# One-hots without factors, rows in two parts, and a router term that no longer crosses GpSimd

## The chip, the cores and the metric

One core of a Trainium2 chip runs the whole kernel; nothing is shared with another core. The metric is the device time of one execution in microseconds, and what is shown is the median of three runs. A profile belongs to one further execution of its own.

## The reference

A single layer of a diffusion backbone over 256 tokens of width 1024, all in float32. First an attention and a spatial-gating branch, joined by an output projection; then 32 experts, of which each token uses four.

```python
x_mid = x + gt1 * rms_norm(mix, g_post_mix[l])            # mix: attention | gating, @ w_out
h2 = modulate(rms_norm(x_mid, g_pre_ffn[l]), sh2, sc2)
logits = xt @ w_router + b_router                         # (256, 32)
top_logits, top_idx = lax.top_k(logits, 4)
gates = jax.nn.softmax(top_logits, axis=-1)
...
gu = xb @ w_gate_up[e] + b_gate_up[e]                     # xb: the rows of expert e
gate = jnp.minimum(gate, 7.0); up = jnp.clip(up, -7.0, 7.0)
act = (up + 1) * gate * jax.nn.sigmoid(1.702 * gate)
y_rows = (act @ w_down[e] + b_down[e]) * row_gate
y = jax.ops.segment_sum(y_rows, row_tok)                  # back to tokens
x_new = x_mid + gt2 * rms_norm(y, g_post_ffn[l])
```

All expert weights are read from HBM in every execution: 12.58 MB for each expert, about 403 MB in all.

## The kernel before, in words

**The part ahead of the experts** (0 to about 203 us) has its order written out by hand: `PLAN` is a list of words, each of which issues the next piece of a step (a generator). `broadcasts` (word `bcast`) spreads four rows of constants over the 128 partitions with GpSimd's partition broadcast. `router_terms` (word `rterms`) multiplies the shift `sh2` with the router's weights `wr` into one row (tile `brt` in PSUM), adds the router's bias into `brow`, and has GpSimd spread that row over the partitions (SBUF tile `brt`). `bparts` is a chain of small GpSimd steps that splits the experts' biases into parts (`braw`, `bgu`). `ra` is the inverse root of the attention rows' mean square: the matmul `oss` sums the squares, `rav` takes it over, and GpSimd works out the root. The output projection's results (`wo`) are scaled by `ra` on VectorE into `yacc`, which then frees `wo`'s PSUM bank.

**The experts** run in a loop `for e in range(NE)`. Their weights come through a ring of ten slots of SBUF (`slot`, `load_more`), six loads of 2 MB for each expert, issued on SyncE's queue (SP) as slots come free. One expert has 64 row slots. Two experts share a gather and a combine:

- `pair_one_hots` writes for 2 x 64 slots a one-hot matrix `oh` of tokens by slots, and `ohg`, the same with the gates in place of ones. In `oh` the ones are replaced by `zx`, the inverse root of the token's mean square.
- `gather_pair` (at the odd expert) multiplies the token rows `xs` by `oh` in float32, eight blocks of 128 columns, two token halves each, into `gx`, and `modulate` makes `xT` of it.
- `gu_chunk` (four for each expert) is the gate and up product, `swiglu` the activation (`g`, `sg`, `u`), `to_ff` the transposition `aT`, and `down` the product `py`, which is copied into `ye`, half by ScalarE and half by VectorE.
- `turn` (at the even expert) transposes `ohg` into `ohT` (`slots_to_partitions`, PSUM bank 2, the bank that `py` uses behind it) and combines the pair before: `combine` multiplies `ohT` with `ye` (`cb`, four float32 matmuls) and `add_y` adds into `yacc`.

TensorE runs its instructions in program order: at the even expert the pieces are `ohT`, `cb`, `aT`, the biases, `py`. An expert with more than 64 rows takes a branch (`rows_left`) through `more_start`, `more_chunk` and `more_down`; with these inputs that happens twice, at about 442 and 949 us. The last pair is handled apart (`project`, `add_up`), and the residual rows `xs` are added at the end.

Matmuls on float32 data leave two records each in the trace; those on data declared `FR` (float32r: the same 32 bits, one pass) leave one.

Of the kernel before, what the change touches and what calls it, by code (L numbers as in the profile page):

```python
# [20 lines left out]
P = 128  # L21
# [24 lines left out]
PLAN = """  # L46
first first bcast first@5 first first first split0 xin00@2 xin01@7 xin01 mod0@0 xin00 split0 xin10@3 first xin10
split0 mod0 mod0@7 split0 acc@6 bias mod0 bias bias bias bias bias split0 mod0 xin11@7 bias proj0 mod0 ada2 xin11
# [34 lines left out]
def kernel(  # L83
# [115 lines left out]
    load(vrow, vecs)  # L199
    xs = keep.tile([P, 2, D], F32, name="xs")  # L200
    for t in range(2):
# [662 lines left out]
    brt = pre.tile([P, NE], F32, name="brt")  # L864
    gt1 = keep.tile([P, D], F32, tag="ye", name="gt1")

# [295 lines left out]
    def modulate(xT, pb, k0, nk, w):  # L1162
# [3 lines left out]
        tt(xT[:, k0:k0 + nk, :], xT[:, k0:k0 + nk, :], bc(sh2[:, k0:k0 + nk].unsqueeze(2), shp), ADD, eng=G)  # L1166

    def one_hots(e, s0, oh, ohg):
        for t in range(2):
            if s0 == 0:  # L1170
                if oh(t) is not None:
                    ts(oh(t), iota[:, 0:oh(t).shape[-1]], pos1[:, t, e:e + 1], zx[:, t:t + 1], ALU.is_equal, MUL)
                ts(ohg(t), iota[:, 0:ohg(t).shape[-1]], pos1[:, t, e:e + 1], gate[:, t, e:e + 1], ALU.is_equal, MUL)
            else:
                w = ohg(t).shape[-1]
                ts(oh(t), iota[:, 0:w], float(s0), pos1[:, t, e:e + 1], ADD, ALU.is_equal)
                ts(ohg(t), oh(t), gate[:, t, e:e + 1])
                ts(oh(t), oh(t), zx[:, t:t + 1])

    def pair_one_hots(p):  # L1180
        oh = None if p == 0 else mt("oh", [P, 2, P])
        ohg = mt("ohg", [P, 2, P])
        for j in range(2):
            c = slice(SL * j, SL * j + SL)
            one_hots(2 * p + j, 0, lambda t: oh[:, t, c] if oh is not None else None, lambda t: ohg[:, t, c])
        return oh, ohg

    def gather_pair(oh):
        xT = mt("xT", [P, KD, P])
# [53 lines left out]

    def down(w, aT, ye):
# [26 lines left out]
    def more_start(e, s0, i, xT, pgu):  # L1271
        ohs = mt("oh", [P, 2, 2, SM])
        oh, ohg = ohs[:, 0], ohs[:, 1]
        one_hots(e, s0, lambda t: oh[:, t, :], lambda t: ohg[:, t, :])
        pb = bank(4, "gx")
        for k in range(KD):
            for t in range(2):
                PE.matmul(pb[:, SM * k:SM * k + SM], lhsT=xs[:, t, P * k:P * k + P], rhs=oh[:, t, :],
                          start=t == 0, stop=t == 1)
        modulate(xT, pb, 0, KD, SM)  # L1280
# [97 lines left out]

    def project(c0, n, j, w, aT, ye, b):

# [5 lines left out]
        yield  # L1386
        rows = ye[SL * j:SL * j + SL]
        S.copy(rows[:, c0:c0 + n], py[0][0:64, 0:n])
        V.tensor_copy(out=rows[:, c0 + n:c0 + 2 * n], in_=py[1][64:128, 0:n])
        yield  # L1390

    def add_up(c, i, ohT, ye, yg, b):
        for t in range(2):
            pb = bank(b + t, "cb")[:, 0:c.stop - c.start]
            PE.matmul(pb, lhsT=ohT[:, t, :], rhs=ye[:, c], start=True, stop=True)
            add_y(t, c, pb)
# [38 lines left out]
    ye = ohT = None  # L1435
    counts_of = {}
# [7 lines left out]
    def turn(p, banks):  # L1444
# [7 lines left out]
        return next(turned), keep.tile([P, D], F32, tag="ye", name=f"ye{p}")  # L1452

# [5 lines left out]
    for e in range(NE):  # L1459
# [14 lines left out]
        for c in range(4):  # L1474
# [4 lines left out]
            if c == 1 and last:  # L1479
                aT0 = to_ff(u0, scr[:, 0:512].rearrange("p (q s) -> p q s", q=4))  # L1480
                ohT, ye = turn(p, (6, 7, 0, 1))
            if c == 2 and not last:
                counts_of[e + 1] = count(e + 1, counted)
        if e == NE - 2:
            scr = slot(order[cursor[0] % NSLOT], "scr")
            cursor[0] += 1
            w0, more0, cv0 = w, more, cv
            continue
# [4 lines left out]
        if j == 0:  # L1493
            ohT, ye = turn(p, (4, 5, 6, 7))
        elif not last:
# [3 lines left out]
        if last:  # L1499

            first = project(0, 512, 0, w0, aT0, ye, 0)
            next(first)
# [8 lines left out]
        down_rest(e, w, more, cv)  # L1511
        down(w, aT, ye[SL * j:SL * j + SL])
        load_more(2)
# [83 lines left out]
```

## Time and profile before

| | |
|---|---|
| median of 3 runs | 1160.65 us (1160.21 to 1161.82) |
| profiled execution | 1159.75 us |
| its span, first to last instruction | 1157.9 us |
| mean granted TensorE clock | 0.966 of 2.4 GHz |
| PE busy | 1066.3 us (92%) |
| VectorE (DVE) / ScalarE (ACT) / GpSimd (POOL) busy | 343.6 / 150.1 / 110.4 us |
| DMA | 446.21 MB, 385 GB/s over the span, 425 to 428 GB/s in its flat stretches |

The span's ends, 1.85 us in all, belong to the execution but to no instruction. All engines' shares are averages over a part with little DMA, a long part in which both DMA and PE are nearly full, and a tail after the last weights. A record line gives the start, the busy time, engine, source line, operation, output <- inputs, shape and how many instructions it groups; what stands in brackets is the idle time ahead of it and what ended it. `L117` is the recording helper that issues nearly every instruction, so the tiles' names tell the places apart.

### The profile page before, as it was taken

To read this page: it belongs to the slowest core of one execution; us is meant where nothing else is said; L and a number is where in the kernel's file an instruction comes from. 1 tells how busy PE (TensorE), PEld (TensorE's weight loads), DVE (VectorE), ACT (ScalarE), POOL (GpSimd) and SP (SyncE) were. 2 spreads that over 40 slices of the span, in tenths; PEclk is the share of its full clock that TensorE was granted. 3 is DMA by queue.
4 is the path that set the end of the run, shared out by engine and by line. 5 is a ranking of instruction groups with operands and counts; after the bars stand their busy time and mean duration, and the time that the engine had idled before them with its cause. 6 is when DMAs were issued, how large, how long until landed. Compare 5 with 4: busy or idle time off the path is not lost. (4 is left out here: it accounts for less than half of the span.)

```text
span 1157.9 us, 14247 instructions
## 1 busy us (share of the span) xinstructions
PE 1066.3 (92%) x5653; PEld 526.6 (45%) x5653; DVE 343.6 (30%) x763; ACT 150.1 (13%) x308; POOL 110.4 (10%) x199
## 2 busy tenths in 40 slices
PE   6998979999999997999999999989998988999985
PEld 5865536343535443444453535343434352353534
DVE  4698534112121321322222121212121221312123
ACT  4654112111000000000000000000000000100011
POOL 2235252000000000000000000000000000000001
PEclk9998988999999998999999999999999998899998
DMA  9976866999999999989999999999999999899961
GB/s 375 369 282 247 352 218 234 408 428 424 425 426 427 425 426 428 424 354 426 428 424 428 421 428 423 426 426 425 426 426 426 426 426 428 359 430 423 423 256 38
DMA packets 36574, 446.21 MB, mean 385 GB/s; under 512 B 4081, under 2 KB 4321, under 8 KB 6657
## 3 DMA queue, kind: packets, MB, share of 16 engines
q1 hardware_dynamic: 36450, 444.47, 92.0%
q8 instruction: 88, 1.44, 0.5%
q14 instruction: 36, 0.29, 0.1%
HBM read 443.41 MB, written 1.05 MB: 384 GB/s over the span
## 5 line engine op out<-in xcount | busy, mean ns | idle before, releaser
L117 PE MATMUL pg<-we,xT 128*64 128x512 f32 x872 | 233.1, 603 | 22.7 <-DMA we<-in_w_gate_up_dram 18.2
L117 PE MATMUL pu<-we,xT 128*64 128x512 f32 x872 | 231.6, 599 | 0.0
L117 PE MATMUL py<-we,g 128*64 128x512 f32 x848 | 193.1, 601 | 4.2 <-ACTq L1338 3.8
L117 PEld LDWEIGHTS pg<-we,xT 128*64 128x64 f32 x872 | 68.1, 138 | 148.1 <-issue 120.7
L117 PEld LDWEIGHTS py<-we,g 128*64 128x64 f32 x848 | 89.6, 138 | 94.0 <-issue 79.7
L117 DVE TENSOR_SCALAR g<-pg 128x512 f32<-128x512 f32 x31 | 21.4, 692 | 366.5 <-PE pg L117 353.5
L117 PEld LDWEIGHTS pu<-we,xT 128*64 128x64 f32 x872 | 72.8, 138 | 116.9 <-issue 116.9
L117 DVE COPY ye<-py 64x512 f32<-64x512 f32 (+2 forms) x36 | 22.9, 635 | 273.4 <-ACTq L1338 208.8
L117 POOL TENSOR_TENSOR xT<-xT,sh 128x512 f32<-128x512 f32 x30 | 31.2, 1040 | 754.7 <-DVE xT L117 746.3
L117 ACT ACTIVATE sg<-g 128x512 f32<-128x512 f32 (+1 forms) x34 | 21.4, 630 | 449.0 <-DVE g L117 449.0
L117 PEld LDWEIGHTS gx<-oh,xs 128*128 128x128 f32 x544 | 67.3, 205 | 18.6 <-PE pg L117 9.7
L117 PE MATMUL gx<-oh,xs 128*128 128x128 f32 (+1 forms) x544 | 70.6, 290 | 4.9 <-DVE oh L117 4.9
L117 PE MATMUL cb<-ye,ohT 128*128 128x512 f32 (+1 forms) x132 | 57.9, 581 | 0.5 <-DVE ye L117 0.5
L117 ACT COPY ye<-py 64x512 f32<-64x512 f32 (+2 forms) x36 | 19.1, 531 | 250.7 <-PE py L117 250.7
L117 DVE TENSOR_TENSOR yacc<-cb,yacc 128x512 f32<-128x512 f32 (+1 forms) x74 | 46.1, 670 | 12.4 <-PE cb L117 12.4
L117 PE MATMUL wo<-wo,proj 128*128 128x512 f32 x64 | 31.5, 632 | 8.5 <-DVE proj L117 8.5
L117 PEld LDWEIGHTS cb<-ye,ohT 128*128 128x128 f32 x132 | 23.7, 190 | 23.0 <-issue 15.2
L117 DVE TENSOR_TENSOR xT<-gx,a 128x512 f32<-128x512 f32 x30 | 20.6, 688 | 14.3 <-PE gx L117 14.3
L117 ACT COPY g<-aT 128x512 f32<-128x512 f32 x30 | 17.6, 586 | 51.4 <-PE aT L117 48.1
L117 DVE TENSOR_TENSOR u<-u,sg 128x512 f32<-128x512 f32 x32 | 22.2, 692 | 3.8 <-ACT sg L117 0.5
L117 DVE TENSOR_SCALAR u<-pu 128x512 f32<-128x512 f32 x31 | 21.4, 692 | 5.5 <-PE pu L117 5.5
L117 DVE SCALAR_TENSOR_TENSOR u<-u,g 128x512 f32<-128x512 f32 x32 | 22.1, 692 | 1.1
(389 smaller groups left out, 1009.5 us busy)
## 6 DMA issues: line engine op xcount, KB each, us to landing
we<-in_w_gate_up_dram SPq DMA_DIRECT2D x116, 2048.0 KB, 27.1
we<-in_w_down_dram SPq DMA_DIRECT2D x53, 2048.0 KB, 27.4
we_a<-in_w_gate_up_dram SPq DMA_DIRECT2D x12, 1024.0 KB, 23.5
we_b<-in_w_gate_up_dram SPq DMA_DIRECT2D x12, 1024.0 KB, 21.9
ada<-in_w_ada_dram SPq DMA_DIRECT2D x8, 1024.0 KB, 11.0
adb<-in_w_adb_dram SPq DMA_DIRECT2D x4, 2048.0 KB, 8.2
win<-in_w_in_dram SPq DMA_DIRECT2D x8, 896.0 KB, 11.5
we_a<-in_w_down_dram SPq DMA_DIRECT2D x7, 1024.0 KB, 22.2
```

The lines of the kernel that those rows point to most:

```text
L117: inst = call(*args, **kwargs)
```

## The change

The token rows are scaled by `zx` once (`split_rows`) and kept as a high part `xhi` (rounded to float32r) and the rest `xlo`; the one-hots hold exact ones, so that the gather runs as one-pass matmuls, two for each one before. In the combine the gate is taken out of `ohT` too: a row sum of `ohg` transposed gives `gs`, `weigh` multiplies it into `ye` while that is written as a high and a low part, and `ohT` is compared to zero, now on VectorE. The residual `xr` is rebuilt from both parts near the end. The four partition broadcasts of constants become broadcast loads on SP's queue, issued later; `router_terms` multiplies with `sh2` spread over 128 columns, so that every partition gets the sum directly. `ye`, `xT` and `gt1` change the tags that they share.

```diff
@@ PLAN
-first first bcast first@5 first first ...
+first first first@5 first first ...
-... proj4 win3 cnorm split4 lws
+... proj4 win3 cnorm split4 lws bcast
-bparts sgu0 ... soft10 soft10 pt013 bparts sgu0 rterms
+bparts sgu0 ... soft10 soft10 pt013 bparts sgu0 ...
     def broadcasts():
-        G.partition_broadcast(rsk, rowt[:, R_BR:R_BR + 40])
-        G.partition_broadcast(bkv, rowt[:, R_BIN + 512:R_BIN + 768])
-        G.partition_broadcast(lng, rowt[:, R_LNG:R_LNG + 512])
-        G.partition_broadcast(lnb, rowt[:, R_LNB:R_LNB + 512])
-        G.partition_broadcast(bob, rowt[:, R_BOUT:R_BOUT + D])
+        for dst, c, n in ((rsk, R_BR, 40), (bkv, R_BIN + 512, 256), (s9[:, 2048:3072], R_LNG, 1024), (bob, R_BOUT, D)):
+            load(dst, rows[:, c:c + n].to_broadcast([P, n]))
     def router_terms():
         pb = psum_tile("brt")
         for k in range(KD):
-            PE.matmul(pb[0:1, 0:NE], lhsT=sh2[:, k:k + 1], rhs=wr[:, k, :], start=k == 0, stop=k == KD - 1)
+            PE.matmul(pb[:, 0:NE], lhsT=bc(sh2[:, k:k + 1], [P, P]), rhs=wr[:, k, :], start=k == 0, stop=k == KD - 1)
         yield
-        row = tmp("brow", [1, NE], bufs=1)
-        tt(row, pb[0:1, 0:NE], rsk[0:1, 0:NE], ADD)
-        yield
-        G.partition_broadcast(brt, row)
+        tt(brt, pb[:, 0:NE], rsk[:, 0:NE], ADD)
+    def split_rows():
+        for t in range(2):
+            S.activation(xs[:, t, :], xs[:, t, :], AF.Copy, scale=zx[:, t:t + 1])
+            S.copy(xhi[:, t, :], xs[:, t, :])
+            tt(xlo[:, t, :], xs[:, t, :], xhi[:, t, :].bitcast(F32), SUB, eng=G)
+    def gather(pb, k, oh):
+        for t in range(2):
+            for i, x2 in enumerate((xhi, xlo)):
+                PE.matmul(pb, lhsT=x2[:, t, P * k:P * k + P], rhs=oh[:, t, :], start=t + i == 0, stop=t + i == 2)
     def gather_pair(oh):
...
-            for t in range(2):
-                PE.matmul(pb[k // 4][:, P * (k % 4):P * (k % 4) + P], lhsT=xs[:, t, P * k:P * k + P], rhs=oh[:, t, :],
-                          start=t == 0, stop=t == 1)
+            gather(pb[k // 4][:, P * (k % 4):P * (k % 4) + P], k, oh)
     def slots_to_partitions(ohg):
...
-        ohT = mt("ohT", [P, 2, P])
-        S.copy(ohT, po[:, 0:2 * P].rearrange("p (t s) -> p t s", t=2))
-        yield ohT
+        ohT = mt("ohT", [P, 2, P], dt=FR)
+        ts(ohT, po[:, 0:2 * P].rearrange("p (t s) -> p t s", t=2), 0.0, op0=ALU.not_equal)
+        gs = mt("gs", [P, 1], bufs=2)
+        S.activation(mt("sg", [P, 512])[:, 0:2 * P], po[:, 0:2 * P], AF.Copy, accum_out=gs)
+        yield ohT, gs
+    def weigh(ye, j, c, py, gs):
+        r = slice(SL * j, SL * j + SL)
+        S.activation(ye[r, 0, c], py, AF.Copy, scale=gs[r, 0:1])
+        stt(ye[r, 1, c], py, gs[r, 0:1], ye[r, 0, c].bitcast(F32), MUL, SUB)
     def down(w, aT, ye, j, gs):
...
-        S.copy(ye[:, 0:512], py[0:64, :])
-        V.tensor_copy(out=ye[:, 512:1024], in_=py[64:128, :])
+        for n in range(2):
+            weigh(ye, j, halves[n], py[64 * n:64 * n + 64, :], gs)
     def combine(ohT, ye, banks):
...
-                PE.matmul(pb, lhsT=ohT[:, t, :], rhs=ye[:, c], start=True, stop=True)
+                for h in range(2):
+                    PE.matmul(pb, lhsT=ohT[:, t, :], rhs=ye[:, h, c], start=h == 0, stop=h == 1)
@@ in the loop
+    split_rows()
     _, ohg = pair_one_hots(0)
@@ at e == NE - 2
+            for t in range(2):
+                tt(xr[:, t, :], xhi[:, t, :].bitcast(F32), xlo[:, t, :].bitcast(F32), ADD, eng=G)
+                S.activation(xr[:, t, :], xr[:, t, :], AF.Copy, scale=rz[:, t:t + 1])
```

GpSimd's program around the router's row, before: the steps of `bparts` stand on both sides of the broadcast `brt<-brow`, and an unnamed `ISA` row stands ahead of and behind it.

```order
L117 TENSOR_SCALAR rs_1261<-rs_1261 128x1 x6
L117 CAST bgu<-braw 96x512
L117 TENSOR_TENSOR braw<-braw,bgu 64x512
L117 ISA
L117 ISA brt<-brow_1236 128x32
L117 CAST bgu<-braw 64x512
L117 ISA
L117 TENSOR_TENSOR braw<-braw,bgu 32x512
```

The same place after:

```order
L116 TENSOR_SCALAR rs_1259<-rs_1259 128x1 x6
L116 CAST bgu<-braw 96x512
L116 TENSOR_TENSOR braw<-braw,bgu 64x512
L116 CAST bgu<-braw 64x512
L116 TENSOR_TENSOR braw<-braw,bgu 32x512
```

The broadcast and both `ISA` rows are gone, and nothing else moved there.

TensorE at a turn (`ohT` is the transposition, `cb` the combine of the pair before, `aT` the transposed activation), before:

```order
L117 MATMUL ohT_2350<-cs,ohg_2004 128x128 x2
L117 MATMUL cb_2353<-ye_1883,ohT_1881 128x512
L117 MATMUL cb_2355<-ye_1883,ohT_1881 128x512
L117 MATMUL cb_2357<-ye_1883,ohT_1881 128x512
L117 MATMUL cb_2359<-ye_1883,ohT_1881 128x512
L117 MATMUL aT_2368<-cs,u_2346 128x128 x4
```

After, each of the four is a pair of one-pass matmuls (high and low part):

```order
L116 MATMUL ohT_2408<-cs,ohg_2029 128x128 x2
L116 MATMUL cb_2411<-ye_1891,ohT_1886 128x512 x2
L116 MATMUL cb_2414<-ye_1891,ohT_1886 128x512 x2
L116 MATMUL cb_2417<-ye_1891,ohT_1886 128x512 x2
L116 MATMUL cb_2420<-ye_1891,ohT_1886 128x512 x2
L116 MATMUL aT_2433<-cs,u_2404 128x128 x4
```

The order is kept; the count of instructions doubles, while each is no longer run in two passes.

VectorE at the same turn, after: behind the activation's last product and the four additions of `add_y` now stands the step that writes `ohT` out of PSUM; before, ScalarE did that, and the branch followed the additions at once.

```order
L116 TENSOR_TENSOR u_2404<-u_2404,sg_2402 128x512
L116 TENSOR_TENSOR yacc<-cb_2411,yacc 128x512
L116 TENSOR_TENSOR yacc<-cb_2414,yacc 128x512
L116 TENSOR_TENSOR yacc<-cb_2417,yacc 128x512
L116 TENSOR_TENSOR yacc<-cb_2420,yacc 128x512
L116 TENSOR_SCALAR ohT_2427<-ohT_2408 128x256
L1350 COMPARE_AND_BRANCH
```

What moved is the release of PSUM bank 2, which `py` needs: it now stands behind the additions.

## Rows read from the trace of the kernel before

**Rows 1.** Windows: us, busy (x) of PE, PEld, DVE, ACT, POOL; clock, DMA share, GB/s.

```profile
300.00:400.00 100.00, 97.99 (x464) 44.38 (x464) 21.61 (x43) 7.29 (x13) 4.04 (x4) 1.00 1.01 425
...
490.00:500.00 10.00, 9.98 (x34) 4.95 (x34) 2.77 (x4) 0.05 (x1) 0.00 (x0) 0.83 0.67 256
...
1000.00:1010.00 10.00, 9.84 (x35) 2.73 (x35) 0.69 (x1) 0.16 (x1) 0.00 (x0) 0.76 0.66 251
```

**Rows 2.** Waits of SP's queue: engine waited for, us in total, times, longest.

```profile
SPq L117 <- PE gu L117: 27.2, 4, 20.3
```

**Rows 3.** Timeline of POOL around the router's row.

```profile
130.75 0.31 POOL L117 PARTITION_BROADCAST brt<-brow  x1 [10.05 <-issue]
...
142.34 1.15 POOL L117 TENSOR_TENSOR braw<-braw,bgu 32x512 f32<-32x512 f32 x1 [10.77 <-issue]
...
147.83 0.53 POOL L117 TENSOR_SCALAR ra<-rav 128x1 f32<-128x1 f32 x2
```

**Rows 4.** Timeline of DVE, the same stretch.

```profile
130.41 0.16 DVE L117 TENSOR_SCALAR rav<-oss 128x1 f32<-128x1 f32 x1 [0.19 <-PE oss L117]
...
151.14 1.41 DVE L117 SCALAR_TENSOR_TENSOR yacc<-wo,ra,yacc 128x512 f32<-128x512 f32 x2 [9.45 <-POOL ra L117]
```

**Rows 5.** Timeline of PE, 114 to 166 us.

```profile
114.05 0.63 PE L117 MATMUL brt<-wr,sh 128*1 128x32 f32 x16
...
142.61 1.08 PE L117 MATMUL accpv<-PT,proj 128*64 128x256 f32 x8
...
153.21 3.78 PE L117 MATMUL wo<-wo,proj 128*128 128x512 f32 x4 [8.48 <-DVE proj L117]
156.92 1.72 PE L117 MATMUL accpv<-PT,proj 128*64 128x256 f32 x8
...
163.18 1.98 PE L117 MATMUL wo<-wo,proj 128*128 128x512 f32 x4
165.00 0.95 PE L117 MATMUL oss<-ones,osq 128*128 128x1 f32 x8
```

**Rows 6.** Window 150 to 160 us, columns as in the first group.

```profile
150.00:160.00 10.00, 6.79 (x19) 2.89 (x20) 5.13 (x9) 1.33 (x4) 4.84 (x13) 0.59 0.59 211
```

**Rows 7.** Timeline at a gather.

```profile
701.13 3.65 PEld L117 LDWEIGHTS gx<-oh,xs 128*128 128x128 f32 x32 [0.81 <-PE pg L117]
...
702.76 0.69 DVE L117 TENSOR_TENSOR u<-u,sg 128x512 f32<-128x512 f32 x1
...
704.81 0.60 PE L117 MATMUL aT<-cs,u 128*128 128x128 f32 x4
```

**Rows 8.** Weight loads by shape: busy us, mean ns, idle before.

```profile
L117 PEld LDWEIGHTS cb<-ye,ohT 128*128 128x128 f32 x132 | 23.7, 190 | 23.0 <-issue 15.2 <-PE cb L117 3.6 <-ACT sg L117 3.1
...
L117 PEld LDWEIGHTS accsu<-wsp,tmp 128*128 128x128 f32 x18 | 3.4, 189 | 0.0
```

**Rows 9.** Timeline at a turn.

```profile
727.81 3.60 PE L117 MATMUL cb<-ye,ohT 128*128 128x512 f32 x8
...
729.78 2.48 DVE L117 TENSOR_TENSOR yacc<-cb,yacc 128x512 f32<-128x512 f32 x4
...
732.88 7.09 PE L117 MATMUL py<-we,g 128*64 128x512 f32 x32 [0.48 <-ACTq L1338]
```

**Rows 10.** Group of GpSimd by line and tile: busy us, mean ns, idle before.

```profile
L117 POOL TENSOR_TENSOR xT<-xT,sh 128x512 f32<-128x512 f32 x30 | 31.2, 1040 | 754.7 <-DVE xT L117 746.3
```

**Rows 11.** Timeline of PE: two turns, 52.8 us apart.

```profile
376.25 3.60 PE L117 MATMUL cb<-ye,ohT 128*128 128x512 f32 x8
...
429.04 3.60 PE L117 MATMUL cb<-ye,ohT 128*128 128x512 f32 x8
```

**Rows 12.** Timeline of PE: the gather of a branch, and the tail.

```profile
443.92 5.68 PE L117 MATMUL gx<-oh,xs 128*128 128x32 f32 x30 [0.29 <-DVE oh L117]
...
1131.52 5.13 PE L117 MATMUL py<-we,scr 128*64 128x128 f32 x64 [5.49 <-PEq L1416]
...
1137.16 1.96 PE L117 MATMUL cb<-ye,ohT 128*128 128x512 f32 x4 [0.50 <-DVE ye L117]
```

More of the change, by code (lines that the diff above doesn't have):

```diff
@@ L46 @@
 PLAN = """
-first first bcast first@5 first first first split0 xin00@2 xin01@7 xin01 mod0@0 xin00 split0 xin10@3 first xin10
+first first first@5 first first first split0 xin00@2 xin01@7 xin01 mod0@0 xin00 split0 xin10@3 first xin10
 split0 mod0 mod0@7 split0 acc@6 bias mod0 bias bias bias bias bias split0 mod0 xin11@7 bias proj0 mod0 ada2 xin11
@@ L199 @@
     load(vrow, vecs)
-    xs = keep.tile([P, 2, D], F32, name="xs")
+    xs = keep.tile([P, 2, D], F32, tag="xs", name="xs")
     for t in range(2):
@@ L864 @@
     brt = pre.tile([P, NE], F32, name="brt")
-    gt1 = keep.tile([P, D], F32, tag="ye", name="gt1")
+    gt1 = keep.tile([P, D], F32, tag="xT", name="gt1")
     def rest_mod():
@@ L1166, in modulate @@
         tt(xT[:, k0:k0 + nk, :], xT[:, k0:k0 + nk, :], bc(sh2[:, k0:k0 + nk].unsqueeze(2), shp), ADD, eng=G)
+    xhi = keep.tile([P, 2, D], FR, name="xhi")
+    xlo = moe.tile([P, 2, D], FR, name="xlo")
+    def split_rows():
[7 more added lines that the diff above has]
+                PE.matmul(pb, lhsT=x2[:, t, P * k:P * k + P], rhs=oh[:, t, :], start=t + i == 0, stop=t + i == 2)
     def one_hots(e, s0, oh, ohg):
@@ L1176, in one_hots @@
                 ts(oh(t), iota[:, 0:w], float(s0), pos1[:, t, e:e + 1], ADD, ALU.is_equal)
-                ts(ohg(t), oh(t), gate[:, t, e:e + 1])
-                ts(oh(t), oh(t), zx[:, t:t + 1])
+                ts(ohg(t), oh(t).bitcast(F32), gate[:, t, e:e + 1])
     def pair_one_hots(p):
-        oh = None if p == 0 else mt("oh", [P, 2, P])
+        oh = None if p == 0 else mt("oh", [P, 2, P], dt=FR)
         ohg = mt("ohg", [P, 2, P])
@@ L1242, in wd, with down @@
         return w[4 + f // 4][f % 4 // 2][:, f % 2, c0:c0 + n]
-    def down(w, aT, ye):
+    def down(w, aT, ye, j, gs):
         py = bank(2, "py")
@@ L1271, in more_start @@
     def more_start(e, s0, i, xT, pgu):
-        ohs = mt("oh", [P, 2, 2, SM])
-        oh, ohg = ohs[:, 0], ohs[:, 1]
+        oh, ohg = mt("oh", [P, 2, SM], dt=FR), mt("ohm", [P, 2, SM])
         one_hots(e, s0, lambda t: oh[:, t, :], lambda t: ohg[:, t, :])
@@ L1276, in more_start @@
         for k in range(KD):
-            for t in range(2):
-                PE.matmul(pb[:, SM * k:SM * k + SM], lhsT=xs[:, t, P * k:P * k + P], rhs=oh[:, t, :],
-                          start=t == 0, stop=t == 1)
+            gather(pb[:, SM * k:SM * k + SM], k, oh)
         modulate(xT, pb, 0, KD, SM)
@@ L1377, in gate2, with project @@
             yield
-    def project(c0, n, j, w, aT, ye, b):
+    def project(c0, n, j, w, aT, ye, gs, b):
         py, n = [bank(b + h, "py") for h in range(2)], n // 2
@@ L1386, in project @@
         yield
-        rows = ye[SL * j:SL * j + SL]
-        S.copy(rows[:, c0:c0 + n], py[0][0:64, 0:n])
-        V.tensor_copy(out=rows[:, c0 + n:c0 + 2 * n], in_=py[1][64:128, 0:n])
+        for h in range(2):
+            weigh(ye, j, slice(c0 + n * h, c0 + n * h + n), py[h][64 * h:64 * h + 64, 0:n], gs)
         yield
@@ L1394, in add_up @@
             pb = bank(b + t, "cb")[:, 0:c.stop - c.start]
-            PE.matmul(pb, lhsT=ohT[:, t, :], rhs=ye[:, c], start=True, stop=True)
+            for h in range(2):
+                PE.matmul(pb, lhsT=ohT[:, t, :], rhs=ye[:, h, c], start=h == 0, stop=h == 1)
             add_y(t, c, pb)
@@ L1433 @@
     xT, pgu = xT0, [tiles["gu", b] for b in range(2)]
+    split_rows()
     _, ohg = pair_one_hots(0)
-    ye = ohT = None
+    ye = ohT = gs = None
     counts_of = {}
@@ L1451, in turn @@
             next(summed, None)
-        return next(turned), keep.tile([P, D], F32, tag="ye", name=f"ye{p}")
+        return *next(turned), keep.tile([P, 2, D], FR, tag="xs", name=f"ye{p}")
     def down_rest(e, w, more, cv):
@@ L1480 @@
                 aT0 = to_ff(u0, scr[:, 0:512].rearrange("p (q s) -> p q s", q=4))
-                ohT, ye = turn(p, (6, 7, 0, 1))
+                ohT, gs, ye = turn(p, (6, 7, 0, 1))
             if c == 2 and not last:
@@ L1484 @@
         if e == NE - 2:
-            scr = slot(order[cursor[0] % NSLOT], "scr")
-            cursor[0] += 1
+            scr, xr = (slot(order[(cursor[0] + i) % NSLOT], "scr") for i in range(2))
+            cursor[0] += 2
+            xr = xr[:, 0:2 * D].rearrange("p (t d) -> p t d", t=2)
+            rz = mt("rz", [P, 2])
+            V.reciprocal(out=rz, in_=zx)
+            for t in range(2):
+                tt(xr[:, t, :], xhi[:, t, :].bitcast(F32), xlo[:, t, :].bitcast(F32), ADD, eng=G)
+                S.activation(xr[:, t, :], xr[:, t, :], AF.Copy, scale=rz[:, t:t + 1])
             w0, more0, cv0 = w, more, cv
@@ L1493 @@
         if j == 0:
-            ohT, ye = turn(p, (4, 5, 6, 7))
+            ohT, gs, ye = turn(p, (4, 5, 6, 7))
         elif not last:
@@ L1499 @@
         if last:
-            first = project(0, 512, 0, w0, aT0, ye, 0)
+            first = project(0, 512, 0, w0, aT0, ye, gs, 0)
             next(first)
@@ L1511 @@
         down_rest(e, w, more, cv)
-        down(w, aT, ye[SL * j:SL * j + SL])
+        down(w, aT, ye, j, gs)
         load_more(2)
@@ L1518 @@
     yg = scr[:, 1536:1536 + 2 * D].rearrange("p (t d) -> p t d", t=2)
-    for step in (project(0, 256, 1, w, aT1, ye, 2), project(256, 256, 1, w, aT1, ye, 0), add_up(halves[0], 0, ohT, ye, yg, 4),
-                 project(512, 512, 0, w0, aT0, ye, 2), project(512, 256, 1, w, aT1, ye, 0),
-                 project(768, 256, 1, w, aT1, ye, 2), add_up(slice(512, 768), 1, ohT, ye, yg, 6),
+    for step in (project(0, 256, 1, w, aT1, ye, gs, 2), project(256, 256, 1, w, aT1, ye, gs, 0), add_up(halves[0], 0, ohT, ye, yg, 4),
+                 project(512, 512, 0, w0, aT0, ye, gs, 2), project(512, 256, 1, w, aT1, ye, gs, 0),
+                 project(768, 256, 1, w, aT1, ye, gs, 2), add_up(slice(512, 768), 1, ohT, ye, yg, 6),
                  add_up(slice(768, 1024), 2, ohT, ye, yg, 4)):
@@ L1536 @@
         for c in halves:
-            stt(xs[:, t, c], yg[:, t, c], zy[t][0][:, 0:1], xs[:, t, c], MUL, ADD)
-            load(out[P * t:P * t + P, c], xs[:, t, c])
+            stt(xr[:, t, c], yg[:, t, c], zy[t][0][:, 0:1], xr[:, t, c], MUL, ADD)
+            load(out[P * t:P * t + P, c], xr[:, t, c])
 def shape_constants():
@@ L1589 @@
     ins = {k: a(v) for k, v in ins.items()}
-    nc = bacc.Bacc("TRN2", target_bir_lowering=False, num_devices=1)
+    nc = bacc.Bacc("TRN2", target_bir_lowering=False, num_devices=1, dynamic_dma_scratch_size=1024)
     aps = {k: nc.dram_tensor(f"in_{k}_dram", v.shape, F32, kind="ExternalInput").ap() for k, v in ins.items()}
```

9 lines of the change are left out of this document (4 added, 5 removed).

## The prediction

> **What bounds the kernel now.** I read the windows first. Through the experts the DMA moves 425 GB/s while PE is busy 97.99 of 100 us [rows 1]: two engines are nearly full, and a step shorter on PE is worth something only where PE is late. It is late twice. After each branch for an expert of more than 64 rows the load stream sinks, to 256 GB/s in 490 to 500 us and 251 GB/s in 1000 to 1010: the ring is full because PE hasn't freed slots. Lost loading: (425 − 256)/425 × 10 = 4.0 us and (425 − 251)/425 × 10 = 4.1 us. Behind the second one nothing stands but PE's own chain and the tail, so PE sets the end from there; between them the load stream does. How near they run is seen at two turns that follow each other: PE needs 52.8 us for two experts (429.04 − 376.25) where the stream needs 25.17 MB at 425 GB/s = 59.2 us [rows 1, 11].
>
> The part ahead of the experts counts in full: SP's queue stands 20.3 us for the first gate-up matmuls to free a slot [rows 2]. An expert loop that begins t us earlier starts the stream t us earlier, and all behind it follows. So I looked at what delays PE in that part. There is one large hole, and it ends in a chain of three engines. GpSimd stands idle 10.05 us ahead of its broadcast `brt` and 10.77 us ahead of the next step but one, in both cases for nothing that the trace shows ("issue") [rows 3]; the order ahead has an unnamed `ISA` row at both places, which I take for the change of GpSimd's program. Meanwhile `rav` has been ready since 130.41 + 0.16, but `ra` comes only at 147.83 + 0.53 [rows 3, 4]. VectorE waits 9.45 us for it, and PE 8.48 us for VectorE to free `wo`'s bank [rows 4, 5].
>
> **The change part by part.**
>
> *The router's row without GpSimd.* Both pauses go with the broadcast. POOL's other steps then run 20 us sooner, `ra` is there before 131 + 2, and the next `wo` need not wait: −8.48. Behind the hole PE runs slower: the granted clock in 150 to 160 us is 0.59 [rows 6], and four `wo` take 3.78 us at 153.21 where four take 1.98 at 163.18; eight `accpv` take 1.72 where they took 1.08 at 142.61 [rows 5]. These are the two levels, 1.2 and 2.4 GHz, and PE had stood idle just before. Without the hole, −1.80 and −0.64. The matmul `brt` now has 128 columns of weights instead of one. Its 16 records took 0.63 us [rows 5]; eight records of `oss`, with 128-column loads and one column moving, take 0.95 [rows 5], so 16 take 1.9: +1.27, on a PE that is dense there. Sum −9.65. Bounds: at worst part of the wait returns as the wait for the mean square's own chain (`ra`'s remaining steps on POOL and VectorE, some 3 us): −6.5; at best the further slow matmuls behind 158 recover too: −11. I take −9.6.
>
> *The constants as loads.* 1.2 MB on SP's queue, ahead of which the queue waits for a slot anyway; at 385 GB/s 3 us of transfer while the stream isn't the limit. The first user of a constant comes well behind the last of these loads in the hand-written order. 0; without that cover 3 us at most.
>
> *The gather.* Before: 16 float32 matmuls, 32 records; after: 32 one-pass matmuls, 32 records. What one costs depends on whether the weights' load or the streaming is the limit. A gather's 32 loads take 3.65 us, 114 ns apart [rows 7]; eight with a single moving column are 0.95/8 = 119 ns apart [rows 5], so the load alone makes this pace. A load for one-pass data, `accsu`, takes 189 ns against 190 for float32 [rows 8]. So 32 records cost the same as before: 0. Bounds: at 80 ns, the pace of `py` in the tail (5.13/64, but with 64-column loads [rows 12]), 32 × 34 ns = 1.1 us would go; more than that can't, since `aT` then waits for `u` (ready at 703.45, `aT` at 704.81 [rows 7]). Above it nothing: no row shows a one-pass matmul slower than its float32 twin.
>
> The Trainium skill ("TensorE: Matmul & The Clock Gate", § Back-to-back issue gap) gives about 81 ns for a matmul of 128 columns in a sustained run. By it a gather would take 2.6 us, and the sum would be near that of the first rival; the pace of 119 ns for 128-column loads on this trace speaks for the slower one, and the same page's § LDWEIGHTS, by which a load takes its columns at 1.2 GHz (107 ns for 128), speaks for it too.
>
> *The combine at a turn.* Four float32 matmuls in 3.60 us become eight one-pass ones; a one-pass matmul with 512 columns takes 7.09/32 = 0.222 us (`py` [rows 9]), so 1.8. That is 1.8 us less for `cb`, but `aT` behind it needs `u`, and `py` behind that needs PSUM bank 2. `ohT` now leaves this bank on VectorE behind the four additions: 729.78 + 2.48 + about 0.4 (half of a 512-column step of 0.69 [rows 7]) = 732.7, and `py` began at 732.88 [rows 9]. So the gain ends in a wait, at every turn: 0, bounds −1.8 (if the additions start enough earlier) and +0.5. Only the last turn, whose banks are others and where no `py` follows, keeps it: −1.6.
>
> *Weighing.* `down` writes `ye` with four steps in place of two, beside PE's next expert: 0; it would cost 0.5 us per expert if the next pair needed `ye` at once. The two branches and the tail do need it: +0.2 for the branches, −0.2 in the tail, where four records of `cb` take 1.96 us [rows 12] and become four of 0.222 (−1.0) against longer evacuations (+0.8).
>
> *`split_rows` and `xr`.* At the loop's start and at the 31st expert GpSimd and ScalarE get new steps: four GpSimd passes of 1024 columns at 2 × 1.04 us [rows 10]. At the start the first gather stands behind two experts' gate-up chunks: 0. At the 31st they stand ahead of a sigmoid: 0 to 0.8, I take +0.3.
>
> Sum: −9.6 − 1.6 + 0.2 − 0.2 + 0.3 = −10.9. The profiled execution took 1159.75 us (its span 1157.9), so 1148.85; the median lies 0.9 above it, so **1149.5**.
>
> **The rivals.**
>
> *A, the gather gains.* If one-pass loads run 80 ns apart, every gather is 1.1 us shorter. Up to the first stall there are four, and the branch's gather (30 records in 5.68 us [rows 12]) would halve, −2.9: 7.3 us, more than the 4.0 us of the stall, which vanishes. From the second branch on −2.9 and two gathers −2.3. 1149.5 − 4.0 − 5.2 = **1140.3**. For it: `py`'s 80 ns; against: equal load durations, `oss`.
>
> *B, another wait takes the hole's place.* `wo` needs probabilities, `accpv`, VectorE: if the next of them is late by 4 us or so, or PE's clock sinks there anyway, the change is worth 5.6 instead of 9.6: **1153.7**, at worst 1158.
>
> *C, slower.* PE's clock falls where it does less. In 490 to 500 us it was granted 0.83 [rows 1], while PE waited on and off: 3.4 us at the lower level, which cost 1.7. If one-pass gathers, with half the streaming behind each load, bring such a drop each, then four pairs before the first stall and three behind the second pay 7 × 1.7 = 11.9: 1161.4; with turns too, 1173. From 1.9 us for each of these pairs it is slower than before. Against it: the clock is 1.00 over 300 to 400 us [rows 1], though gathers, bound by their loads today too, lie in it.
>
> *D, the change doesn't do what it says.* If the idle 10 us belong to something else than the broadcast, they stay, and only the combine's −1.6 and +0.3 are left: about **1159.5**. Against it: both pauses sit exactly where the order has the `ISA` rows.
>
> **How the numbers follow.** My forecast 0.58, A 0.14, B 0.15, C 0.08, D 0.05. The forecast's own range is 1147 to 1154 (the hole's −6.5 to −11, the turns, `xr`). The range 1140 to 1157 takes in A and most of B and leaves out C, D and parts of the rest. A difference counts from 0.2%, 2.3 us, about what a measurement of this kernel can tell from none: faster holds the forecast, A and nearly all of B: 0.86; D and the edge of B and C within it: 0.07; most of C slower: 0.07.
>
> **What the profile will show.** Right: no POOL idle of 10 us behind 120 us; `ra` before 135; no PE wait of 8 us for `proj`, `wo` at 2 us for four throughout; the first gate-up slot freed some 9.6 us earlier; 32 gather loads in 3.6 us as before; `cb` in 1.8 us with a wait of about 1.5 us ahead of `aT` or `py`; the two sinks in the stream still there. Wrong: gather loads in 2.6 us (A), a new wait on PE between 135 and 160 (B), a clock below 0.95 in windows with a gather (C), the pauses elsewhere on POOL (D). The forecast falls most easily with the turn: if `py` no longer begins at the same place, each late pair gains up to 1.8 us more, or loses if VectorE is slower than thought.

## The result, and the profile after

The changed kernel is slower: 1176.78 us (median of 4 runs, 1175.62 to 1177.93) against 1160.43 us (4 runs, 1159.65 to 1161.82), a ratio of 1.0140 with a 95% interval of 1.0122 to 1.0157. The profiled execution has a span of 1175.9 us, and its mean granted clock went from 0.966 to 0.942. I had forecast 1149.5 us and gave "slower" 7 in 100.

The windows of the changed kernel, with the columns of [rows 1]:

```profile
300.00:400.00 100.00, 93.49 (x430) 40.41 (x428) 24.30 (x48) 9.83 (x18) 2.08 (x2) 0.95 1.01 426
...
470.00:480.00 10.00, 10.00 (x42) 3.24 (x40) 0.00 (x0) 0.00 (x0) 0.00 (x0) 0.85 0.54 192
490.00:500.00 10.00, 8.94 (x61) 3.89 (x53) 3.60 (x6) 1.31 (x3) 0.00 (x0) 0.85 0.52 220
```

In 300 to 400 us PE is busy 93.49 us where it was 97.99, and the clock is 0.95 where it was 1.00. The stream still runs at 426 GB/s there; the bill comes behind the first branch, where it sinks to 192 and 220 GB/s. Summed over the ten-microsecond windows under 420 GB/s from 200 to 1100 us, the time lost against 425 GB/s is 25.6 us; before it was 12.5. The waits of PE say who holds it up (engine waited for: us in total, times, longest). `ACTq`, `DVEq` and `PEq` are the instruction sequencers of ScalarE, VectorE and PE, and L1350 is the `if` of the branch for an expert of more than 64 rows:

```profile
PE py L116 <- ACTq L1350: 34.1, 13, 2.6
...
PE pu L116 <- ACTq L1350: 5.9, 1, 5.9
PE py L116 <- PEq L1428: 5.5, 1, 5.5
```

The first row is new in size: 13 waits of 2.6 us, one at each turn between the first and the last that has no branch taken, where `py` had waited 0.48 us [rows 9]. The second is new altogether. The third, in the tail, was there before [rows 12]. One turn, on PE, VectorE and ScalarE in that order:

```profile
576.22 2.09 PE L116 MATMUL cb<-ye,ohT 128*128 128x512 f32 x8
578.41 0.66 PE L116 MATMUL aT<-cs,u 128*128 128x128 f32 x4
...
582.24 8.78 PE L116 MATMUL py<-we,g 128*64 128x512 f32 x32 [2.62 <-ACTq L1350]
...
577.66 0.69 DVE L116 TENSOR_TENSOR u<-u,sg 128x512 f32<-128x512 f32 x1
578.27 2.48 DVE L116 TENSOR_TENSOR yacc<-cb,yacc 128x512 f32<-128x512 f32 x4
580.66 0.41 DVE L116 TENSOR_SCALAR ohT<-ohT 128x256 fp32r<-128x256 f32 x1
...
576.08 0.63 ACT L116 ACTIVATE sg<-g 128x512 f32<-128x512 f32 x1 [12.02 <-DVE g L116]
581.19 0.38 ACT L116 ACTIVATE sg<-ohT 128x256 f32<-128x256 f32 x1 [4.48 <-DVEq L1350]
581.47 0.19 ACT L116 ACTIVATION_READ_ACCUMULATOR sg<-ohT 128x1 f32 x1
581.56 0.58 ACT L116 COPY g<-aT 128x512 f32<-128x512 f32 x1
```

Read it backwards from `py`. It needs `g`, the copy of `aT`, which starts at 581.56 although `aT` was done at 579.07. ScalarE stood 4.48 us in front of the row sum `sg<-ohT` (that is `gs`), and began it when VectorE had ended `ohT` (580.66 + 0.41); VectorE had the four additions in front of `ohT`. So the combine is 1.5 us shorter, and `py` begins 6.02 us after `cb` instead of 5.07. And `py` itself takes 8.78 us where it took 7.09; of the 13 turns one keeps 7.09, nine take 8.5 to 8.8 and three about 10.0. From `cb` to the end of `py` this turn takes 14.80 us, 12.16 before.

The second new wait lies in the last pair, shown on GpSimd, ScalarE and PE:

```profile
1113.10 5.09 POOL L116 TENSOR_TENSOR scr<-xhi,xlo 128x1024 f32<-128x1024 f32 x2 [20.89 <-PE pu L116]
...
1115.48 1.15 ACT L116 ACTIVATE scr<-scr,rz 128x1024 f32<-128x1024 f32 x1 [14.50 <-POOL scr L116]
1118.23 1.15 ACT L116 ACTIVATE scr<-scr,rz 128x1024 f32<-128x1024 f32 x1 [1.60 <-POOL scr L116]
1119.57 0.63 ACT L116 ACTIVATE sg<-g 128x512 f32<-128x512 f32 x1 [0.19 <-ACTq L1350]
...
1113.17 0.41 PE L116 MATMUL pg<-bgu,e 96*64 96x512 bf16 x2
1119.47 0.64 PE L116 MATMUL pu<-bgu,e 96*64 96x512 bf16 x2 [5.89 <-ACTq L1350]
1119.85 1.97 PE L116 MATMUL pg<-we,xT 128*64 128x512 f32 x4
```

GpSimd's additions for `xr` write into a ring slot (`scr`) that the last gate-up product frees only at 1113.1. ScalarE's two scalings wait for them, and its branch and sigmoid stand behind; PE's bias matmul waits for that branch 5.89 us and then runs three groups at the lower level (1.91 to 1.97 us instead of 1.06).

The front did what it was meant to. PE there:

```profile
112.32 1.97 PE L116 MATMUL brt<-wr,sh 128*128 128x32 f32 x16
...
129.78 0.73 PE L116 MATMUL PT<-cs,probs 128*128 128x128 f32 x4 [1.02 <-DVE proj L116]
...
132.66 3.76 PE L116 MATMUL wo<-wo,proj 128*128 128x512 f32 x4
136.21 1.91 PE L116 MATMUL PT<-cs,probs 128*128 128x128 f32 x8
...
158.19 0.95 PE L116 MATMUL oss<-ones,osq 128*128 128x1 f32 x8
```

The wait of 8.48 us for `proj` [rows 5] is gone, and the second `oss` starts at 158.19 instead of 165.00, 6.8 us earlier. The slow `wo` is not gone: it stands at 132.66 now. The first gate-up product starts at 186.46 instead of 192.62, 6.2 us earlier.

### The profile page after: what moved, and what is told of

It is laid out like the page before. It is cut to its first block, busy times and chain, and to the rows that moved or that the text cites. A ratio compares the mean times of both kernels' runs of the same rounds, so it can differ in the third digit from the quotient of the medians.

```text
span 1175.9 us, 14375 instructions
## 1 busy us (share of the span) xinstructions
PE 1070.3 (91%) x5653; PEld 531.9 (45%) x5653; DVE 373.0 (32%) x812; ACT 183.3 (16%) x366; POOL 116.4 (10%) x197
## 5 line engine op out<-in xcount | busy, mean ns | idle before, releaser
L116 PE MATMUL py<-we,g 128*64 128x512 f32 x848 | 208.9, 643 | 26.2 <-ACTq L1350 26.2
L116 DVE SCALAR_TENSOR_TENSOR ye<-py,gs,ye 64x512 fp32r<-64x512 f32 (+2 forms) x72 | 49.7, 691 | 330.1 <-ACT ye L116 311.0
L116 PEld LDWEIGHTS pg<-we,xT 128*64 128x64 f32 x872 | 71.7, 138 | 124.1 <-issue 122.9
L116 ACT ACTIVATE ye<-py,gs 64x512 fp32r<-64x512 f32 (+2 forms) x72 | 45.7, 635 | 293.6 <-PE py L116 146.0
L116 PE MATMUL gx<-oh,xhi 128*128 128x128 f32 (+1 forms) x272 | 66.3, 287 | 6.7 <-DVE oh L116 6.7
L116 PE MATMUL gx<-oh,xlo 128*128 128x128 f32 (+1 forms) x272 | 65.7, 286 | 0.0
L116 PEld LDWEIGHTS gx<-oh,xhi 128*128 128x128 f32 x272 | 55.8, 205 | 19.9 <-PE pg L116 10.5
L116 PEld LDWEIGHTS gx<-oh,xlo 128*128 128x128 f32 x272 | 56.0, 206 | 0.0
L116 PE MATMUL cb<-ye,ohT 128*128 128x512 f32 (+1 forms) x132 | 34.5, 400 | 0.9 <-ACT ye L116 0.8
L116 PE MATMUL py<-we_a,g 128*64 128x512 f32 x56 | 20.4, 840 | 7.9 <-ACTq L1350 7.9
```

What stands on the lines that cost most here:

```text
L116: inst = call(*args, **kwargs)
```

## The experiments

Theory Q (queue): PE waits at the turns for what stands in program order on ScalarE and VectorE ahead of what it needs, and idle time there costs the clock as well. Rival K (clock): the one-pass matmuls themselves, which stream less behind each weight load, lower the clock; this is the third rival of the prediction. Theory X is the wait for `xr`. Times below are medians, ratios are to the kernel before run beside them. Its own median moved from 1158.11 to 1160.43 us between series, so two runs are compared by their ratios, as us of 1160. How long `py` takes at a turn is read from one execution of each run.

**1. `ohT` ahead of the additions.**

```diff
             next(summed)
+            out = next(turned)
             next(summed, None)
+        else:
+            out = next(turned)
-        return *next(turned), ...
+        return *out, ...
```

> The changed kernel with one step moved: VectorE writes ohT before the four additions of the combine instead of behind them; nothing else. Theory Q (queue): ScalarE's row sum gs waits for VectorE's ohT, and behind gs on ScalarE stand the copy of aT and the branch, for which py waits; PE's 2.6 us at each turn and the slower half of py behind it (8.78 us instead of 7.09) then go together. By Q py begins about 3.8 us after cb (6.0 now), takes 7.1 us, the stream's losses behind the first branch fall from some 16 us to under 6, and the time is 1158 to 1164 us. Rival K (clock): the one-pass combine itself, which streams less behind each weight load, lowers PE's clock; the wait goes, but py stays near 8.8 us, and the time is 1167 to 1172.

Measured: 1165.55 us, ratio 1.0059 (1.0040 to 1.0078), 9.4 us less than the changed kernel (11.2 by the medians). Neither theory's picture came: `py` begins 5.3 us after `cb`, not 3.8, and is still slow (8.5 to 8.8 us) at 11 of the 13 turns. The wait became shorter, but another engine ended it (below).

**2. `xr` later.** The additions and scalings moved behind the last expert's first sigmoid and bias matmuls, the scalings to GpSimd.

```diff
-                S.activation(xr[:, t, :], xr[:, t, :], AF.Copy, scale=rz[:, t:t + 1])
+                ts(xr[:, t, :], xr[:, t, :], rz[:, t:t + 1], eng=G)
```

> The changed kernel with the rebuilding of the residual xr moved behind the last expert's first sigmoid and its scaling taken from ScalarE to GpSimd; nothing else. Theory X: ScalarE's two scalings wait for GpSimd's additions, which wait for a ring slot, and the sigmoid, the branch and so PE's next bias matmul stand behind them (5.9 us, and then three slow groups of matmuls). By X that wait goes, and the time falls by 8 to 9 us, to 1167 to 1169. Rival: the wait is for the branch itself, as another wait of the tail is; then it stays and the time is within 2 us of 1176.8.

Measured: 1169.03 us, ratio 1.0084 (1.0065 to 1.0102), 6.5 us less (7.8 by the medians). The wait of 5.9 us is gone, and `pu`'s bias follows `pg`'s at once. X holds.

**3. Both edits.**

> Both edits of the two runs before it. By Q and X together the stream has hardly any loss left behind the first branch and the tail is as long as before the change: 1146 to 1154 us, below the kernel before. By K the sum stays at 1157 to 1164.

Measured: 1158.42 us, ratio 0.9993 (0.9977 to 1.0009): the same as before the change, above what Q and X together had given, inside what was given for K. A turn shows why (PE, then VectorE, then ScalarE):

```profile
571.13 2.09 PE L116 MATMUL cb<-ye,ohT 128*128 128x512 f32 x8
...
576.46 8.62 PE L116 MATMUL py<-we,g 128*64 128x512 f32 x32 [1.93 <-DVEq L1350]
...
573.26 0.42 DVE L116 TENSOR_SCALAR ohT<-ohT 128x256 fp32r<-128x256 f32 x1
573.60 2.48 DVE L116 TENSOR_TENSOR yacc<-cb,yacc 128x512 f32<-128x512 f32 x4
...
574.15 0.58 ACT L116 COPY g<-aT 128x512 f32<-128x512 f32 x1
```

ScalarE has `g` ready at 574.73 and bank 2 is free, yet PE waits for `DVEq L1350`: VectorE's branch, which stands behind the additions (573.60 + 2.48). The branch's body uses bank 2 for its own `py`, so the `py` behind the branch waits for VectorE to pass it, taken or not.

**4. The front alone.** The kernel before with the new `broadcasts`, `router_terms` and `PLAN`; gather, combine and `xr` as before.

> The kernel before with only the part ahead of the experts changed: constants by broadcast loads, the router's row summed in all partitions, no partition broadcast. The gather, the combine and xr are as before. The prediction gave this part 9.6 us (1150.8); the changed kernel's trace has the expert loop 6.2 to 6.8 us earlier, so now 1153 to 1155 us. If the earlier loop is taken back by the load stream, 1160.

Measured: 1151.51 us, ratio 0.9926 (0.9901 to 0.9951): 8.1 us faster by the medians, 8.6 by the ratio, and faster than the 1153 to 1155 expected. The forecast's term of 9.6 us was right in kind. The interval (5.7 to 11.5 us) can't tell it from 8.1; the trace can: the first gate-up product starts at 185.83, 6.8 us earlier than before the change.

**5. The branch's `py` in another bank**, on top of both edits:

```diff
     def more_down(w, i):
-        py = bank(2, "py")
+        py = bank(4, "py")
```

> The kernel with both edits, and the branch's own py moved from PSUM bank 2 to bank 4, so that a branch not taken no longer ties the next py to VectorE's branch, which stands behind the four additions (1.9 us of waiting per turn, and py at 8.6 us). Theory Q (py is held by what its bank and the branch tie it to, and the idle time costs the clock): py begins about 0.3 us after aT is copied, 3.7 us after cb (5.3 with both edits, 5.1 in the kernel before) and takes 7.1 us; a turn from cb to the end of py takes 10.8 to 11.2 us (12.2 before the change, 14.8 after it); 1140 to 1149 us. Rival K (the one-pass matmuls themselves lower the clock): py begins sooner, but keeps 8.4 us or more; 1150 to 1157 us.

Measured: 1152.45 us, ratio 0.9938 (0.9914 to 0.9963). The turn is what Q said:

```profile
561.10 2.09 PE L116 MATMUL cb<-ye,ohT 128*128 128x512 f32 x8
...
564.87 7.09 PE L116 MATMUL py<-we,g 128*64 128x512 f32 x32 [0.37 <-DVE yacc L116]
```

3.77 us from `cb` to `py`, 7.09 us for `py` at 12 of 13 turns and 7.38 at one, 10.86 us in all. K as I had put it falls: the one-pass matmuls are the same, and `py` keeps its pace. The time alone would not have told: it lies in the range given for K and above the one given for Q.

**6. The front alone, with that bank.**

> The kernel before with the part ahead of the experts changed and the branch's py in bank 4; gather and combine in float32 as before. It measures beside the first run what the one-pass gather and combine are worth without the waits. py waits 0.5 us less at a turn at most; 1147 to 1152 us. If the one-pass forms pay, the first run is 3 to 8 us below this one; if not, they are equal.

Measured: 1150.92 us, ratio 0.9935 (0.9915 to 0.9955), equal to run 5. With every new wait at the turns taken away, the one-pass gather and combine make no difference to the time that can be measured. PE's waits for weights in run 5 (first row) and here tell where part of a turn's 1.2 us went:

```profile
PE pg L116 <- DMA we<-in_w_gate_up_dram: 26.0, 22, 2.0
```

```profile
PE pg L116 <- DMA we<-in_w_gate_up_dram: 16.2, 15, 2.8
```

PE is early and waits for the stream. Another part came through and was lost again behind the loop. From the first gate-up product to the last turn's `cb` the profiled execution of run 5 takes 913.7 us (186.70 to 1100.44) and this one 918.6 (181.18 to 1099.81); from there to the end of the span it is 50.0 us against 46.1. In that tail PE stood at the lower level longer, as 1120 to 1130 us show for run 5 and then here (columns of [rows 1]):

```profile
1120.00:1130.00 10.00, 7.62 (x48) 5.87 (x50) 2.42 (x6) 1.80 (x5) 0.34 (x1) 0.50 0.01 3
```

```profile
1120.00:1130.00 10.00, 9.50 (x92) 7.12 (x90) 1.97 (x4) 1.96 (x6) 2.51 (x2) 0.86 0.01 2
```

Run 3, with the same combine and the old bank, has a tail of 45.1 us. These are single executions, and no run tests what makes run 5's tail longer.

**7 to 9. A wait put into the kernel before.** Two, five or seven VectorE steps that multiply `yacc` by one, behind the additions, with the float32 combine (here the five of run 8):

```diff
             next(summed, None)
+            for i in range(5):
+                ts(yacc[:, i % 2, halves[i // 2 % 2]], yacc[:, i % 2, halves[i // 2 % 2]], 1.0)
```

> The kernel before, with two more VectorE steps of 512 columns (yacc times one) behind the additions of each turn; gather and combine are as before. It makes the wait ahead of py about 1.9 us instead of 0.5. By Q (idle time alone costs the clock): py takes 8.4 us or more, a turn 2.6 to 3.0 us more, and the time is 1168 to 1176 us. By K (a wait alone does nothing, one-pass matmuls do): py stays at 7.1 us, a turn 1.4 us more, 1162 to 1166 us.

> The kernel before with five more VectorE steps (yacc times one, 0.38 us each as the two of the run before showed) behind the additions of each turn: a wait of about 2.0 us ahead of py, as with both edits, but with the float32 combine. By Q (idle time alone costs the clock): py at 8.4 us or more at most turns, a turn near 15.2 us, 1172 to 1182 us. By K (only after one-pass matmuls): py stays at 7.1 us, a turn near 13.7 us, 1165 to 1171 us.

> As the run ahead of it with seven such steps: a wait of about 2.8 us, a little over that of the changed kernel (2.6). By Q py at 8.7 us or more, a turn 16 us or more, 1180 to 1192 us. By K py at 7.1 us, a turn near 14.4 us, 1170 to 1177 us.

Measured: two steps, which took 0.76 us together and not twice 0.69, only brought the wait to 0.84 us; `py` stayed at 7.09 at all turns, 1162.21 us, ratio 1.0027 (1.0008 to 1.0046). This run missed its dose. Five steps: 1169.07 us, ratio 1.0092 (1.0060 to 1.0124). Seven: 1177.53 us, ratio 1.0165 (1.0117 to 1.0212). Two turns of the run with five steps:

```profile
580.83 3.60 PE L117 MATMUL cb<-ye,ohT 128*128 128x512 f32 x8
...
587.26 7.09 PE L117 MATMUL py<-we,g 128*64 128x512 f32 x32 [1.84 <-DVEq L1338]
```

```profile
797.80 3.60 PE L117 MATMUL cb<-ye,ohT 128*128 128x512 f32 x8
...
804.23 8.77 PE L117 MATMUL py<-we,g 128*64 128x512 f32 x32 [1.84 <-DVEq L1338]
```

The same wait, once with the fast `py` and once with the slow one; slow at 4 of 13 turns, and with seven steps (a wait of 2.5 us) at 5 of 13. So a wait alone does cost the clock, but at fewer turns than behind the one-pass combine with a like wait. Q in its bare form ("idle time alone") falls too, and the times lie under what it gave: with five steps in K's range, with seven 0.5 us above it.

**10. `gs` ahead of `ohT`** in the changed kernel, nothing else:

```diff
+        S.activation(mt("sg", [P, 512])[:, 0:2 * P], po[:, 0:2 * P], AF.Copy, accum_out=gs)
         ts(ohT, po[:, 0:2 * P].rearrange("p (t s) -> p t s", t=2), 0.0, op0=ALU.not_equal)
-        S.activation(mt("sg", [P, 512])[:, 0:2 * P], po[:, 0:2 * P], AF.Copy, accum_out=gs)
```

> The changed kernel with ScalarE's row sum gs issued ahead of VectorE's ohT, nothing else. If ScalarE's queue alone held py, the copy of aT is no longer late and py begins 3.7 us after cb, at 7.1 us: 1155 to 1162 us. If VectorE holds it too (ohT behind the additions, and the branch behind ohT), py begins 5.3 to 5.7 us after cb and stays slow: 1163 to 1172 us.

Measured: 1167.1 us, ratio 1.0093 (1.0062 to 1.0124); `py` begins 5.2 us after `cb` and is slow at 10 of 13 turns. VectorE holds it as well; with ScalarE's queue free, 5.5 us of the 16 go by the ratios (9.7 by the medians), not all.

**11 and 12. A long one-pass combine with a wait.** Both edits of run 3; each pair of combine matmuls twice into the same bank (the second run replaces the first), and five VectorE steps behind the additions. Run 12 also gives `ohT` two buffers.

```diff
-                for h in range(2):
+                for h in (0, 1, 0, 1):
                     PE.matmul(pb, lhsT=ohT[:, t, :], rhs=ye[:, h, c], start=h == 0, stop=h == 1)
```

> The kernel with both edits, each pair of one-pass combine matmuls run twice into the same bank (the second run starts the sum anew), so that cb lasts 3.6 us as in float32, and five VectorE steps behind the additions, so that the wait ahead of py is about 2 us as in the float32 run with five steps. If the one-pass form lowers the clock together with a wait, py is slow at 9 or more of 13 turns, as with both edits, and the time is 1172 to 1182 us. If the short combine did it, by leaving PE less work between its pauses, py is slow at 3 to 6 of 13, as in that float32 run, and the time is 1160 to 1170 us.

> As the run before it, which missed its wait (3.9 us where 2 were meant, since the one buffer of ohT was still being read by the longer combine), with two buffers for ohT. cb lasts 3.9 us and the wait ahead of py is about 1.8 to 2.4 us, that of the float32 run with five steps (1.8, slow at 4 of 13 turns). If the one-pass form lowers the clock together with a wait, py is slow at 9 or more of 13, 1172 to 1184 us; if the short combine did, at 3 to 6 of 13, 1160 to 1170 us.

Measured: run 11 took 1206.06 us, ratio 1.0396 (1.0373 to 1.0420), with a wait of 3.9 us and a slow `py` at all 13 turns; since the wait was twice the one meant, it decides nothing between form and length. Run 12 took 1169.62 us, ratio 1.0085 (1.0061 to 1.0109). A turn:

```profile
576.59 3.93 PE L116 MATMUL cb<-ye,ohT 128*128 128x512 f32 x16
...
583.44 7.09 PE L116 MATMUL py<-we,g 128*64 128x512 f32 x32 [1.93 <-DVEq L1350]
```

The wait is like that of run 3 (1.93 to 2.03 us, there 1.85 to 1.93), the matmuls are one-pass, and `py` is slow at 2 of 13 turns, fewer than either theory gave. So the one-pass form by itself isn't what makes many turns slow. What differs from run 3 is the doubled combine, which keeps PE busy 3.93 us instead of 2.09, with the five steps and the second buffer that it needs. The mean granted clocks of all executions lie the same way: 0.949 to 0.960 in run 3, 0.958 to 0.964 in run 12.

| run | `cb`, us | wait ahead of `py`, us | end of `cb` to `py`, us | slow `py`, of 13 turns |
|---|---|---|---|---|
| before | 3.60, float32 | 0.4 to 0.5 | 1.4 | 0 |
| 5: other bank | 2.09, one-pass | 0.3 to 0.4 | 1.6 | 0 |
| 7: before, two steps | 3.60, float32 | 0.8 | 1.8 | 0 |
| 8: before, five steps | 3.60, float32 | 1.8 | 2.8 | 4 |
| 12: twice, two `ohT` | 3.93, one-pass | 1.9 | 2.9 | 2 |
| 10: `gs` first | 2.09, one-pass | 1.8 | 3.1 | 10 |
| 1: `ohT` early | 2.09, one-pass | 1.9 | 3.2 | 11 |
| 3: both edits | 2.09, one-pass | 1.9 | 3.2 | 9 |
| 9: before, seven steps | 3.60, float32 | 2.5 | 3.5 | 5 |
| the changed kernel | 2.09, one-pass | 2.6 | 3.9 | 12 |
| 11: twice | 3.93, one-pass | 3.9 | 4.8 | 13 |

That the wait is needed is shown both ways: taken away (run 5) the slow `py` goes, put in (runs 8 and 9) it comes. What decides at how many turns is not shown. The length of `cb` is one candidate. Another is the whole stretch from the end of `cb` to `py`, with only `aT` and the biases in it: by it the rows stand nearly in order, with run 9 as the exception. And the turns of one execution follow each other at nearly the same distance (54.5 to 54.6 us at many of run 12's), so 13 turns are not 13 independent trials.

The Trainium skill ("TensorE: Matmul & The Clock Gate", § HAM oscillation) tells of a loop in which PE's work between two waits is shorter than the wait, and in which the clock falls back in every round. Runs 3 and 12 don't have that picture: at the turns shown PE had worked 14.1 us without a break ahead of `cb` in both, and the wait was 1.9 us.

## Why the prediction was wrong, point by point

**The turn, the step that failed.** The prediction said that `ohT` leaves bank 2 on VectorE behind the additions, that `py` would begin where it did, and so "the gain ends in a wait, at every turn: 0, bounds −1.8 and +0.5". The gain did end in a wait. But I looked only at the bank. Behind `gs` on ScalarE stand the copy of `aT` and the branch, and I named neither; they make the start of `py` 1 us later than before. And I let the wait cost nothing beyond itself, although [rows 5] show slow `wo` behind a wait: it cost 1.7 us more in `py` at most turns, and 2.9 to 3.0 at three. Together +2.6 us at most turns instead of 0. Moving `ohT` ahead of the additions gave back 9.4 us (run 1 against the changed kernel) and 10.6 (run 3 against run 2), and the bank (run 5 against run 3) 6.4 us.

**`xr`, 0.3 us taken, 0 to 0.8 as bounds.** Mis-sized: 6.5 us (run 2), 7.7 (run 3 against run 1). I had counted GpSimd's and ScalarE's steps but not when they can begin: the slot that they write is freed by the last product of the same expert, so nothing of them lay beside earlier work, and PE's branch stood behind.

**The front, 9.6 us.** Right in mechanism; 8.1 us measured (run 4), 6.8 us at the second `oss`. The hole went, and `brt` took 1.97 us against 1.9 worked out. What failed is the 2.44 us for the clock, as rival B had allowed: the slow `wo` and its neighbour came back at 132.66, behind a pause of 1.02 us. Two readings were off without harm to the chain. `ra` was not there at 147.83 + 0.53, which is the first of its steps, but after the last ones, at 151.10 before and 135.28 after:

```profile
148.91 2.19 POOL L117 TENSOR_SCALAR ra<-ra 128x1 f32<-128x1 f32 x6
```

```profile
132.89 2.39 POOL L116 TENSOR_SCALAR ra<-ra 128x1 f32<-128x1 f32 x6
```

And PE's 8.48 us ended with `proj`, as the row says, which VectorE wrote behind the two steps that free `wo`'s bank.

**The gather, 0.** Right, for the pace. The loads of one gather, first and last of 32:

```profile
605.06 0.19 PEld L116 LDWEIGHTS gx<-oh,xhi 128*128 128x128 f32 x1 [0.81 <-PE pg L116]
...
608.52 0.19 PEld L116 LDWEIGHTS gx<-oh,xlo 128*128 128x128 f32 x1
```

They start (608.52 − 605.06)/31 = 112 ns apart, and all 32 take 3.46 + 0.19 = 3.65 us, to the hundredth what they took before [rows 7]: rival A has no ground. The 81 ns that the Trainium skill ("TensorE: Matmul & The Clock Gate", § Back-to-back issue gap) gives for 128 moving columns aren't seen with 128-column loads here; the measurement decides.

**The last turn, −1.6 us, and weighing.** `cb` took 2.07 us there instead of 3.60, 1.5 us less and close to what was worked out. The four steps of `weigh` show no cost in the loop (run 5 against run 6).

**The sum.** In the ratios' terms of 1160 us: the front −8.6, `xr` +6.5 (run 2), the order of `ohT`, `gs` and the additions with `xr` already moved +10.6, the branch's bank +6.4, and +1.4 (within the intervals) left between runs 5 and 4: +16.3, against +16.2 measured. Each step is the difference of two neighbouring runs, so that the sum closes is no proof of it. The two profiled executions split the difference of their spans (18.0 us) without it: the loop begins 6.2 us earlier, takes 943.6 us to the last turn's `cb` instead of 918.8, of which run 2's edit gives back 8.8, and the tail behind it is 0.7 us shorter. In the prediction's own sum, 1148.85 + 0.9 is 1149.75 and not 1149.5, which changes nothing.

**The rivals.** C had one right place for the loss, the clock at the turns, and a like price (1.7 us a pair), but a cause that the runs refute: run 5 keeps the one-pass matmuls and the fast `py` at the turns. Its 1173 "with turns too" lies near the measured time by luck, since it counts the gathers, whose pace didn't change, and leaves out `xr`. The row that it leaned on shows PE busy 9.98 of 10 us, so PE wasn't waiting on and off in it. What the slow `py` needed was a pause, and a pause was what the forecast itself contained. That pause was priced at zero, and "slower" was left to C alone, with 7 in 100.

## What to carry to other kernels

When a step moves to another engine, list what stands behind the waiting instruction in that engine's program, branches included, and who waits for those; the resource that the step itself holds is only one of the ties. A matmul made shorter in front of a wait doesn't shorten the path: it lengthens the pause, and the work behind a pause may then run at half the clock, so a "free" wait on the engine that sets the time has a price. A branch that is hardly ever taken can still tie the engines that its body uses, through the buffers in it; another bank for the body was worth 6 us here with the one-pass combine (run 5 against run 3) and nothing measurable with the float32 one (run 6 against run 4).

## What the runs showed of the hardware

A pause of 1.8 to 2.1 us on PE was followed by 1.4 to 1.7 us of lost time in the next 32 matmuls at 2 to 4 of 13 turns when 3.6 to 3.9 us of combine stood ahead of it (runs 8 and 12), and at 9 to 11 of 13 when 2.1 us did (runs 1, 3 and 10). Why it strikes some turns and not others of like rows in one execution stays open. VectorE steps that read and write SBUF alone, with one input of 128x512, took 0.42 us each and 0.76 for two in a row (run 7), where the step with two inputs in [rows 7] took 0.69.
